# A chunked delta-rule recurrence inside a projection stage: the triangular inverse multiplied into its operand ahead of the chain, two matmul bursts a chunk in place of three

## The chip, the cores and the metric

The kernel runs on one core of a Trainium2 chip. The metric is the device time of one execution in microseconds; the number quoted is the median of three runs. TensorE (PE in the rows) does the matmuls, VectorE (DVE) and ScalarE (ACT) do elementwise work and empty PSUM, GpSimd (POOL) does small elementwise work, and SyncE (SP) issues the DMAs.

## The reference

One layer of a hybrid encoder on 528 prompt tokens (16 of them learned meta tokens) and 8 x 16 decode tokens, width 2048, all float32. What matters here is head group A, 16 heads of 64:

```python
h = rms_norm(x, norm_mix)
proj = h @ w_in                              # 2048 x 5408
...
def step(S, inp):                            # per head, S is 64 x 64
    r_t, w_t, k_t, v_t, a_t, b_t = inp
    sa = jnp.einsum('bhvk,bhk->bhv', S, a_t)
    S = S * w_t + sa * b_t + v_t * k_t       # outer products
    return S, jnp.einsum('bhvk,bhk->bhv', S, r_t)
...
x = x + concat(group_norm(y) * gate, conv_branch) @ w_out
x = x + (gelu(conv3(u)) * z) @ w_ffn_down    # [u, z] = rms_norm(x) @ w_ffn_up
```

## The kernel before

**Stages.** In order: load and normalise x; the input projection together with both head groups; the output projection; the feed-forward network (up, down), whose rows come from lines 1277 and 1361 (up) and 1581 and 370 (down); the final norm. The large matmuls split every float32 operand into a high and a low part and use three products (weight high x input high, weight high x input low, weight low x input high), all written by line 154 in the first two of these stages.

**The recurrence.** The 16 heads are worked on in 8 pairs; a pair's two heads sit on partitions 0 to 63 and 64 to 127, so that each small matmul is issued twice, once for each head (h = 0, 1). The tokens of a pair form 11 chunks of 64: chunks 0 and 1 are the decode tokens, chunks 2 to 10 the prompt. Within a chunk the recurrence is solved in closed form: with a unit triangular matrix and its inverse T (`tt`), computed ahead by `core_pre`, the state S of the chunk before gives

- z = (masked k a) v + a S, then u = T z (the correction that the chunk's tokens make to each other),
- y = r S + (masked k r) v + (masked b r) u, and the new S = decay (S + k v + b u).

`core(i)` is a generator that does this for pair i. Each of its steps issues a burst of 64x64 matmuls, then yields a number: how many large matmuls have to pass before its next step. Per chunk there are three bursts: one for z (ends with a copy of z by ScalarE into `zs`, line 871), one for u = T z (rows `g<-zs,tt`; copy into `us`, line 878), one for the new S and for y (copy into `S`, line 896). `prep(c0)` makes the masked products and the transposes for two chunks at a time in two PSUM banks; VectorE (lines 783, 784) and ScalarE (785, 786) copy them into the SBUF tile `slot`.

**What sets the order on TensorE.** From the second step of the stage on, TensorE's instructions stand as the program emits them. `tick()` is called after every large matmul; it advances the generators. The stream `st_b` holds the pairs' `core` generators, `st_p` the `core_pre` ones, `st_e` the group norms (`gn_gen`), others the elementwise chains. The other generators prefer to run where the chain has just issued a burst:

```python
while self.items and self.cnt <= 0 and (beside or self.poll or self.cnt <= -WAIT):
...
def tick():
    st_f.tick()
    beside = st_b.tick() or not st_b.items
    for st in streams:
        st.tick(beside)
```

So `beside` is true in the tick in which the chain issued a burst, or where no chain is left; without it another generator's step waits up to `WAIT` large matmuls beyond its own number. The order of the other engines is set by a scheduler at build time, with a bonus (`HPC`) for the chain's copies.

**PSUM.** `mb()` hands out two banks in turn. `prep` takes both; so do each part of `core_pre`, the state update of the decode chunks, the transposes of `gn_gen` (rows `mb<-consts,yb`), and one bank is taken by the squares in `gn_gen` (line 949, ScalarE writes it, VectorE sums it in line 951). Whoever takes a bank waits until its last user's copies are done. The chain itself accumulates in the tile `g`, in banks of its own.

Of the kernel before, what the change touches and what calls it, by code (L numbers as in the profile page):

```python
# [46 lines left out]
WAIT = 6  # L47
# [15 lines left out]
def hymba_stream_kernel(  # L63
# [305 lines left out]
    def mmx(o_, l_, r_, st_, sp_):  # L369
        nc.tensor.matmul(o_, l_, r_, start=st_, stop=sp_, skip_group_check=True)  # L370
# [376 lines left out]
    def core(i):  # L747
# [6 lines left out]
        RB, KA, RK, BT, VT, KT_ = range(6)  # L754

        def prep(c0):

            nch = min(2, NCH - c0)
            pss = [mb(), mb()]
            for z in range(nch):  # L760
                c = c0 + z
                o = 192 * z
                for h in range(2):
                    x, I = hs[h], ident[hs[h], hs[h]]
                    mmx(pss[h][ot[h], o:o + 128], ar[x, c, 3, :], ar[x, c, 0:2, :], z == 0, True)
                for h in range(2):
                    x, I = hs[h], ident[hs[h], hs[h]]
                    mmx(pss[h][x, o:o + 64], ar[x, c, 2, :], ar[x, c, 1, :], z == 0, True)
                for h in range(2):
                    x, I = hs[h], ident[hs[h], hs[h]]  # L770
                    mmx(pss[h][x, o + 64:o + 128], ar[x, c, 2, :], I, False, True)
                for h in range(2):
                    x, I = hs[h], ident[hs[h], hs[h]]
                    mmx(pss[h][ot[h], o + 128:o + 192], ar[x, c, 3, :], I, False, True)
                for h in range(2):
                    x, I = hs[h], ident[hs[h], hs[h]]
                    mmx(pss[h][x, o + 128:o + 192], vv[x, c * 64:c * 64 + 64], I, False, True)
            sl = rw.tile([P, 2, 6, 64], F32, tag="slot", name="slot", bufs=2)
            kind = int(c0 < 2)
            for h in range(2):  # L780
                pv = pss[h][:, 0:192 * nch].rearrange("p (z w t) -> p z w t", w=3, t=64)
                x, y = hs[h], ot[h]
                TT(sl[x, :nch, RB], pv[x, :, 0], mk[x, kind, 1].unsqueeze(1).to_broadcast([64, nch, 64]), ALU.mult)
                TT(sl[x, :nch, KA:KA + 2], pv[y, :, 0:2], mk[y, kind].unsqueeze(1).to_broadcast([64, nch, 2, 64]), ALU.mult)
                act(sl[x, :nch, BT:BT + 2], pv[x, :, 1:3], AF.Copy)
                act(sl[x, :nch, KT_], pv[y, :, 2], AF.Copy)
            slots[c0] = sl
            if c0 == NCH - 1:
                state["jit"] = i


        am = once("am", [P, 2, 576], 0.0)
        for c in range(2):
            for z in range(2):
                nc.gpsimd.tensor_copy(am[:, c, 256 * z:256 * z + 320].rearrange("p (q w) -> p q w", w=80)[:, :, 0:16],
                                      ar[:, c, z, :].rearrange("p (q j) -> p q j", j=16))
# [11 lines left out]
        for c in range(2):  # L808
            for h in range(2):
                mmx(g[hs[h], h, 64 * c:64 * c + 64], sl[hs[h], c, KA], sl[hs[h], c, VT], c == 0, False)  # L810
            for q in range(4):
                for h in range(2):
                    mmx(g[hs[h], h, 64 * c:64 * c + 64], am[hs[h], c, 64 * q:64 * q + 64], s0[hs[h], 4 * c + q, :], False, q == 3)
                for h in range(2):
                    mmx(g[ot[h], h, 64 * c:64 * c + 64], am[hs[h], c, 256 + 64 * q:320 + 64 * q], s0[hs[h], 4 * c + q, :], c == 0 and q == 0, False)
# [13 lines left out]
        for h in range(2):  # L829
            with ALL(offset=HPC):  # L830
                uv = g[hs[h], h, 128:256].rearrange("p (c v) -> p c v", c=2)
                act(us[hs[h]], uv, AF.Copy)
            for c in range(2):
                with ALL(offset=HPC):
                    TT(um[hs[h], c], uv[:, c].unsqueeze(1).to_broadcast([64, 4, 64]),
                       qm[hs[h]].unsqueeze(2).to_broadcast([64, 4, 64]), ALU.mult)
        yield Y_SU
# [17 lines left out]
        for c in range(2, NCH):  # L855
# [13 lines left out]
            for h in range(2):  # L869
# [3 lines left out]
            for h in range(2):  # L873
                mmx(g[hs[h], h, 64:128], tt[hs[h], c, :], zs[hs[h]], True, True)
# [4 lines left out]
            if z == 0 and c + 2 < NCH:  # L879
                prep(c + 2)  # L880
            yield Y_CU
# [11 lines left out]
            S2 = rw.tile([P, 64], F32, tag="S", name="S", bufs=3)  # L893
# [790 lines left out]
```

## Time and profile before

| | |
|---|---|
| median of three runs | 3164.76 us (3161.8 to 3167.85) |
| profiled execution: its own time | 3158.8 us |
| profiled execution: span from first to last instruction | 3157.0 us |
| TensorE busy | 3004.3 us, 95% |
| VectorE, ScalarE, GpSimd busy | 2304.7 (73%), 1484.1 (47%), 422.9 (13%) us |
| mean granted TensorE clock | 0.979 of 2.4 GHz |

The projection stages end at about 1344 us; the chains of the 8 pairs lie between about 293 and 1316 us. From 1344 us on the feed-forward network runs, which the change does not touch. Matmuls are pipelined, so a matmul's own duration in a row is longer than its distance to the next start; for large matmuls in a row the distance between two starts is the time that each one costs.

### The profile page before, as it was taken

The numbers are of one execution on the slowest core, as the hardware profiler recorded it, in microseconds if no ns is written. First come the engines' busy times: TensorE is split into PE (matmuls) and PEld (weight loads), VectorE is DVE, ScalarE is ACT, GpSimd is POOL, SyncE is SP. The second block draws the span as 40 slices with busy tenths as digits, with TensorE's granted clock in tenths as the row PEclk, the third lists the DMA queues.
The fourth block names the chain that finished last, engine by engine and source line by source line (L and its number), as shares of the span: only waits on it lengthen the run. The fifth ranks groups of instructions, "written<-read, shape, count | busy, mean of one in ns | idle before, by whom it ended". The sixth has DMA issues, their size and how long they took to land.

```text
span 3157.0 us, 63878 instructions
## 1 busy us (share of the span) xinstructions
PE 3004.3 (95%) x24566; PEld 2832.7 (90%) x24566; DVE 2304.7 (73%) x4341; ACT 1484.1 (47%) x3226; POOL 422.9 (13%) x848
## 2 busy tenths in 40 slices
PE   8998998999889999999999999999999999999998
PEld 6887887788768788899999999999999999999997
DVE  5778577766755443388888888888888888888877
ACT  6653544435455544464444444444444444444445
POOL 2124224043240321000000000000000000000001
PEclk9999999999879999999999999999999999999999
DMA  4652333143545433363333333333333375334325
GB/s 136 195 160 68 84 90 87 50 110 77 139 112 169 126 103 109 92 185 100 97 103 96 97 97 99 97 94 97 95 100 102 104 232 159 119 112 145 114 90 158
DMA packets 537644, 362.96 MB, mean 115 GB/s; under 512 B 80392, under 2 KB 506540, under 8 KB 536666
## 3 DMA queue, kind: packets, MB, share of 16 engines
q1 hardware_dynamic: 536682, 358.29, 39.0%
q8 instruction: 193, 3.16, 0.4%
q14 instruction: 113, 0.93, 0.1%
q0 software_dynamic: 656, 0.58, 0.1%
HBM read 294.71 MB, written 65.03 MB: 114 GB/s over the span
## 4 chain that ended last, share of the span: by engine, by line
PE 60%; DMA 5%; DVE 4%; POOL 3%; issue 2%; ACT 2%; SPq 1%; DVEq 0%; ACTq 0%; POOLq 0%
PE p_t L1361 20%; PE p_b L1361 15%; PE mm L154 13%; PE wb L370 9%; POOL tp L694 1%; POOL ttmp L692 1%; DMA ra<-in_w_ffn_down_dram 1%; PE mb L370 1%; PE g L370 1%; DMA wst<-in_w_ffn_down_dram 1%; DVE lo L1582 1%; DMA ct<-c_d 1%; DVE wlo L131 1%; PE pss L370 0%; DMA lp<-ld 0%
## 5 line engine op out<-in xcount | busy, mean ns | idle before, releaser
L1277 ACT ACTIVATE hi<-a 128x512 fp32r<-128x512 f32 x528 | 324.0, 630 | 448.7 <-PE p_b L1361 199.0
L154 PE MATMUL mm<-xh,whi 128*128 128x384 f32 (+2 forms) x1344 | 441.3, 328 | 10.4 <-ACT whi L129 8.6
L154 PE MATMUL mm<-xh,wlo 128*128 128x384 f32 (+2 forms) x1344 | 442.6, 330 | 7.1 <-DVE wlo L131 6.8
L1361 PE MATMUL p_t<-ht,hi 128*128 128x322 f32 x1408 | 441.1, 315 | 0.6 <-ACT hi L1277 0.6
L154 PE MATMUL mm<-xl,whi 128*128 128x384 f32 (+2 forms) x1344 | 440.4, 328 | 0.0
L1361 PE MATMUL p_t<-lt,hi 128*128 128x322 f32 x1408 | 436.5, 311 | 0.0
L1278 DVE TENSOR_TENSOR lo<-a,hi 128x512 fp32r<-128x512 f32 x528 | 352.0, 687 | 109.0 <-ACT hi L1277 79.5
L1361 PE MATMUL p_t<-ht,lo 128*128 128x322 f32 x1408 | 423.1, 312 | 0.0
L131 DVE TENSOR_TENSOR wlo<-wst,whi 128x512 fp32r<-128x512 f32 (+2 forms) x332 | 219.7, 662 | 208.3 <-ACT whi L129 186.2
L129 ACT ACTIVATE whi<-wst 128x512 fp32r<-128x512 f32 (+2 forms) x332 | 198.7, 600 | 255.1 <-PE mm L154 173.3
L154 PEld LDWEIGHTS mm<-xh,wlo 128*128 128x128 f32 (+1 forms) x1344 | 259.5, 193 | 21.3 <-DVE wlo L131 12.0
L154 PEld LDWEIGHTS mm<-xh,whi 128*128 128x128 f32 (+1 forms) x1344 | 259.3, 193 | 20.7 <-ACT whi L129 9.4
L1361 PEld LDWEIGHTS p_t<-ht,hi 128*128 128x128 f32 x1408 | 266.6, 189 | 3.2 <-ACT hi L1277 0.9
L154 PEld LDWEIGHTS mm<-xl,whi 128*128 128x128 f32 (+1 forms) x1344 | 260.3, 194 | 8.4 <-issue 1.8
L1361 PEld LDWEIGHTS p_t<-lt,hi 128*128 128x128 f32 x1408 | 266.7, 189 | 0.0
L1361 PEld LDWEIGHTS p_t<-ht,lo 128*128 128x128 f32 x1408 | 263.4, 190 | 0.4 <-DVE lo L1278 0.3
L1361 PE MATMUL p_b<-hb,lo 128*128 128x322 f32 x704 | 223.5, 317 | 0.0
L1361 PE MATMUL p_b<-lb,hi 128*128 128x322 f32 x704 | 219.6, 312 | 0.0
L1361 PE MATMUL p_b<-hb,hi 128*128 128x322 f32 x704 | 218.6, 311 | 0.0
L154 PE MATMUL mm<-g,whi 128*128 128x320 f32 (+2 forms) x960 | 210.3, 313 | 4.9 <-DVE fy L1495 2.4
L370 PE MATMUL wb<-t,hi 128*128 128x320 f32 x928 | 205.7, 310 | 0.0
L1581 ACT ACTIVATE hi<-ra 128x512 fp32r<-128x512 f32 x174 | 110.0, 632 | 195.4 <-PE wb L370 166.7
(515 smaller groups left out, 7164.3 us busy)
## 6 DMA issues: line engine op xcount, KB each, us to landing
a<-in_w_ffn_up_dram SPq DMA_DIRECT2D x352, 256.0 KB
wst<-in_w_in_dram SPq DMA_DIRECT2D x168, 256.0 KB
ra<-in_w_ffn_down_dram SPq DMA_DIRECT2D x58, 512.0 KB
gr<-g_d SPq DMA_DIRECT2D x84, 320.0 KB
wst<-in_w_ffn_down_dram SPq DMA_DIRECT2D x68, 256.0 KB
g_d<-uu SPq DMA_DIRECT2D x44, 320.0 KB
wst<-in_w_out_dram SPq DMA_DIRECT2D x48, 256.0 KB
ld<-lo_d SPq DMA_DIRECT2D x40, 192.0 KB
```

The source lines that it names most:

```text
L129: act(hi[:, :nk, :nc_], st[:, :nk, :nc_], AF.Copy)
L131: TT(lo[:, :nk, :nc_], st[:, :nk, :nc_], hi[:, :nk, :nc_].bitcast(F32), ALU.subtract)
L154: nc.tensor.matmul(o, w_, x_[kk][:, s0:s1], start=(kk == 0 and w_ is h and x_ is ah), stop=(kk == nk - 1 and w_ is l))
L370: nc.tensor.matmul(o_, l_, r_, start=st_, stop=sp_, skip_group_check=True)
L692: nc.gpsimd.tensor_tensor(tv, lp[:, s:s + 1, s + 1:32].to_broadcast([108, J, L]), tp[:, :J, s:s + 1].to_broadcast([108, J, L]), ALU.mult)
L694: nc.gpsimd.tensor_tensor(tp[:, :J, s + 1:32], tp[:, :J, s + 1:32], tv, ALU.add)
L1277: act(hi[:], v_, AF.Copy)
L1278: TT(lo[:], v_, hi[:].bitcast(F32), ALU.subtract)
L1361: nc.tensor.matmul(pr[op], w_[:, c], x_[z], start=(h == 0 and c == 0 and n == 0), stop=(h == 1 and c == 3 and n == 2))
L1581: act(hi[:], src, AF.Copy)
L1582: TT(lo[:], src, hi[:].bitcast(F32), ALU.subtract)
```

## The change

The inverse T is multiplied into a ahead of the chain: a new step `prep2` takes the slot that `prep` filled one chunk earlier, and computes, for two chunks at a time, zv = (masked k a) v and aT = a transposed times T, which two further copies by ScalarE put back into the slot (over KA and into the new field AT). The chain's first burst then gives u directly, u = T zv + aT S, and the burst for z, its copy `zs` and its `yield` are gone. `prep` gets one more transpose per chunk and head (that of a). On even chunks the first burst is followed by `prep` for the chunks two further on, on odd chunks by `prep2` for the next two. `WAIT` goes from 6 to 10. The tile `S` has 2 buffers in place of 3, the slot has 7 fields in place of 6, and the mask tile `am` is laid out flat.

```diff
-WAIT = 6
+WAIT = 10
...
-        RB, KA, RK, BT, VT, KT_ = range(6)
+        RB, KA, RK, BT, VT, AT, KT_ = range(7)
...
+                for d, w, l, r_ in ((1, p, 3, slice(0, 2)), (0, o, 2, 1), (0, o + 64, 2, None), (1, p + 128, 3, None),
+                                    (0, o + 128, -1, None), (0, o + 192, 0, None)):
+                    for h in range(2):
+                        x = hs[h]
+                        if l == 0 and c0 == 0:
+                            continue
...
+            kind, nt = int(c0 < 2), 3 if c0 else 2
...
+                act(sl[x, :nch, BT:BT + nt], px[:, :, 1:1 + nt], AF.Copy)
+                act(sl[x, :nch, KT_], py[:, :, 2], AF.Copy)
...
+        def prep2(c0):
+
+            nch, sl = min(2, NCH - c0), slots[c0]
+            pss = [mb(), mb()]
+            for z in range(nch):
+                for h in range(2):
+                    x = hs[h]
+                    mmx(pss[h][x, 128 * z:128 * z + 64], sl[x, z, KA], sl[x, z, VT], z == 0, True)
+                for h in range(2):
+                    x = hs[h]
+                    mmx(pss[h][x, 128 * z + 64:128 * z + 128], sl[x, z, AT], tt[x, c0 + z, :], False, True)
+            for h in range(2):
+                x = hs[h]
+                pv = pss[h][x, 0:128 * nch].rearrange("p (z w t) -> p z w t", w=2, t=64)
+                act(sl[x, :nch, KA], pv[:, :, 0], AF.Copy)
+                act(sl[x, :nch, AT], pv[:, :, 1], AF.Copy)
...
+        prep2(2)
         yield Y_SU
...
             for h in range(2):
-                mmx(g[hs[h], h, 0:64], sl[hs[h], z, KA], sl[hs[h], z, VT], True, S is None)
+                mmx(g[hs[h], h, 64:128], tt[hs[h], c, :], sl[hs[h], z, KA], True, S is None)
             if S is not None:
                 for h in range(2):
-                    mmx(g[hs[h], h, 0:64], ar[hs[h], c, 0, :], S[hs[h]], False, True)
+                    mmx(g[hs[h], h, 64:128], sl[hs[h], z, AT], S[hs[h]], False, True)
...
-            zs = rw.tile([P, 64], F32, tag="zs", name="zs", bufs=1)
-            for h in range(2):
-                with ALL(offset=HPC):
-                    act(zs[hs[h]], g[hs[h], h, 0:64], AF.Copy)
-            yield Y_C
-            for h in range(2):
-                mmx(g[hs[h], h, 64:128], tt[hs[h], c, :], zs[hs[h]], True, True)
...
-            if z == 0 and c + 2 < NCH:
-                prep(c + 2)
-            yield Y_CU
+            if c + 2 - z < NCH:
+                (prep2 if z else prep)(c + 2 - z)
+            yield Y_C
```

On TensorE, in the program's order before, one chunk of a late pair reads as follows between large matmuls (line 154): the burst for z, seven large matmuls, then the burst `g<-zs,tt` alone (`arbk` holds a and r, `tt` is T; one row of this order is two instructions in the trace).

```order
5748 L370 MATMUL g<-slot 64x64 x2
5749 L370 MATMUL g<-S,arbk_1950 64x64 x4
5750 L154 MATMUL mm<-c2l,whi 128x322
5751 L154 MATMUL mm<-c2h,wlo 128x322
5752 L154 MATMUL mm<-c3h,whi 128x322
5753 L154 MATMUL mm<-c3l,whi 128x322
5754 L154 MATMUL mm<-c3h,wlo 128x322
5755 L154 MATMUL mm<-c0h,whi 128x320
5756 L154 MATMUL mm<-c0l,whi 128x320
5757 L370 MATMUL g<-zs,tt_2585 64x64 x2
5758 L154 MATMUL mm<-c0h,wlo 128x320
```

In the program's order of the changed kernel an odd chunk of the same pair has this burst on TensorE (`mb<-slot` and `mb<-tt,slot` are `prep2`, `mb<-consts,yb` are the transposes of the group norm).

```order
6033 L154 MATMUL mm<-c0l,whi 128x320
6034 L370 MATMUL g<-slot,tt_2623 64x64 x2
6035 L370 MATMUL g<-S,slot 64x64 x2
6036 L370 MATMUL g<-S,arbk_1950 64x64 x2
6037 L370 MATMUL mb<-slot 64x64 x2
6038 L370 MATMUL mb<-tt_2623,slot 64x64 x2
6039 L370 MATMUL mb<-slot 64x64 x2
6040 L370 MATMUL mb<-tt_2623,slot 64x64 x2
6041 L370 MATMUL mb<-consts,yb_14229 64x64 x12
6042 L154 MATMUL mm<-c0h,wlo 128x320
```

The row `g<-zs,tt` with its own place between large matmuls is gone, and the group norm's transposes, which also use the two `mb` banks, now stand directly behind `prep2`.

ScalarE's order around the same place in the changed kernel, from the even chunk's `prep` on (lines 781 and 782 are the copies of `prep`, 801 and 802 those of `prep2`, 956 the squares of the group norm, 903 the copy of S, 885 that of u, 970 the group norm's output).

```order
1222 L781 ACTIVATE slot<-mb 64x2x192
1223 L782 ACTIVATE slot<-mb 64x2x64
1224 L781 ACTIVATE slot<-mb 64x2x192
1225 L782 ACTIVATE slot<-mb 64x2x64
1226 L956 ACTIVATE mb<-yb_14229 128x384
1227 L903 ACTIVATE S<-g,pc 64x64 x2
1228 L959 ACTIVATE gs<-gs,eps 128x6
1229 L885 ACTIVATE us<-g 64x64 x2
1230 L801 ACTIVATE slot<-mb 64x2x64
1231 L802 ACTIVATE slot<-mb 64x2x64
1232 L801 ACTIVATE slot<-mb 64x2x64
1233 L802 ACTIVATE slot<-mb 64x2x64
```

Here the squares (line 956) stand ahead of the copy of S, and the four copies of `prep2` behind the copy of u. Before, at this place of the pair, a copy `zs` stood between the squares and the group norm's square root, and the copy of S before the squares.

## Rows read from the trace of the kernel before

**Rows 1.** The page: TensorE's busy share in 40 equal slices of 79 us, in tenths, and the granted clock in tenths.

```profile
PE   8998998999889999999999999999999999999998
PEclk9999999999879999999999999999999999999999
```

**Rows 2.** Busy time by stretch: the stage with the chains, then the feed-forward network's up part. Columns: stretch, its length, then busy us (instructions) of PE, PEld, DVE, ACT, POOL, the granted clock, DMA share, GB/s.

```profile
237.00:1344.00 1107.00, 1006.86 (x11304) 884.95 (x11302) 656.20 (x1363) 519.11 (x1362) 287.52 (x614) 0.95 0.37 101
1344.00:2538.00 1194.00, 1188.89 (x7979) 1174.97 (x7978) 993.88 (x1736) 542.13 (x961) 63.02 (x96) 1.00 0.35 104
```

**Rows 3.** Who waited for whom, TensorE, 237 to 1344 us. Columns: total us, times, longest.

```profile
PE mb L370 <- ACT slot L786: 15.4, 18, 4.4
PE g L370 <- ACT S L896: 13.8, 10, 8.4
...
PE mm L154 <- DVE wlo L131: 8.4, 16, 1.0
PE mb L370 <- DVE gs L951: 7.2, 2, 3.8
PE mb L370 <- DVE slot L784: 6.5, 7, 1.6
PE g L370 <- ACT zs L871: 4.7, 5, 3.6
```

**Rows 4.** TensorE in order of time, two bursts of a late pair among large matmuls: start us, duration us, instruction, count.

```profile
1292.94 0.31 PE L154 MATMUL mm<-y1h,whi 128*128 128x322 f32 x1
1293.09 0.31 PE L154 MATMUL mm<-y1l,whi 128*128 128x322 f32 x1
1293.33 0.33 PE L370 MATMUL g<-zs,tt 64*64 64x64 f32 x4
1293.59 0.41 PE L154 MATMUL mm<-y1h,wlo 128*128 128x322 f32 x1
1293.84 0.31 PE L154 MATMUL mm<-y2h,whi 128*128 128x322 f32 x1
...
1294.59 0.31 PE L154 MATMUL mm<-y3h,wlo 128*128 128x322 f32 x1
1294.82 0.36 PE L370 MATMUL g<-slot 64*64 64x64 f32 x8
1294.99 0.22 PE L370 MATMUL g<-S,consts 64*64 64x64 f32 x2
1295.01 0.26 PE L370 MATMUL g<-us,slot 64*64 64x64 f32 x2
1295.05 0.23 PE L370 MATMUL g<-S,consts 64*64 64x64 f32 x2
1295.10 0.28 PE L370 MATMUL g<-us,slot 64*64 64x64 f32 x6
1295.32 0.41 PE L154 MATMUL mm<-y0h,whi 128*128 128x320 f32 x1
1295.57 0.31 PE L154 MATMUL mm<-y0l,whi 128*128 128x320 f32 x1
```

**Rows 5.** The instructions that use the tile `zs`: count, duration ns min/median/max, first and last start. (352 of them, because the decode chunks of every pair, which keep their own z step, use the name too: 176 rows of the program's order at two instructions each, 32 of them of the decode chunks.)

```profile
L370 PE MATMUL g<-zs,tt x352: 218/218/366, 303.9 to 1311.9; 64*64 64x64 f32 x176
```

**Rows 6.** ScalarE's groups, 200 to 1360 us: count, then busy us and mean ns of one, then idle before.

```profile
L785 ACT ACTIVATE slot<-mb 64x256 f32<-64x256 f32 (+1 forms) x96 | 34.5, 360 | 47.0 <-DVE slot L784 39.2 <-PE mm L154 2.8 <-PE g L370 2.0
L871 ACT ACTIVATE zs<-g 64x64 f32<-64x64 f32 x144 | 31.2, 217 | 48.0 <-PE g L370 46.4
L786 ACT ACTIVATE slot<-mb 64x128 f32<-64x128 f32 (+1 forms) x96 | 25.3, 263 | 1.2
L949 ACT ACTIVATE mb<-yb 128x384 f32<-128x384 f32 (+1 forms) x16 | 7.3, 459 | 5.3 <-DVE yb L946 5.3
```

**Rows 7.** TensorE in order of time at three places where `core_pre` takes the two `mb` banks directly behind a `prep`: the last matmuls of the first `prep`, then for each place the first matmul behind it. In brackets: idle us before, and who ended it.

```profile
363.39 0.28 PE L370 MATMUL mb<-consts,vv 64*64 64x64 f32 x4
365.53 0.32 PE L370 MATMUL mb<-arbk 64*64 64x64 f32 x2 [1.85 <-ACT slot L786]
...
1029.24 0.47 PE L370 MATMUL mb<-arbk 64*64 64x64 f32 x2 [2.55 <-ACT slot L786]
...
1152.29 0.32 PE L370 MATMUL mb<-arbk 64*64 64x64 f32 x2 [1.63 <-DVE slot L784]
```

**Rows 8.** TensorE in order of time at other waits for the `mb` banks: the second `prep` of a pair, 8 large matmuls behind its first (two rows); a `prep` behind the squares of the group norm (two places); the group norm's transposes, 14 large matmuls behind a `prep`.

```profile
574.95 0.43 PE L370 MATMUL mb<-arbk 64*64 64x128 f32 x2 [1.01 <-DVE slot L784]
575.71 0.32 PE L370 MATMUL mb<-arbk 64*64 64x128 f32 x3 [0.34 <-ACT slot L786]
...
492.25 0.45 PE L370 MATMUL mb<-arbk 64*64 64x128 f32 x3 [3.35 <-DVE gs L951]
...
917.31 0.47 PE L370 MATMUL mb<-arbk 64*64 64x128 f32 x3 [3.82 <-DVE gs L951]
...
927.92 0.47 PE L370 MATMUL mb<-consts,yb 64*64 64x64 f32 x2 [4.37 <-ACT slot L786]
```

**Rows 9.** In order of time from one `prep` to the next chunk's first burst: the last matmuls of the `prep`, ScalarE's copy of S, and the burst that waited for it.

```profile
596.11 0.28 PE L370 MATMUL mb<-consts,vv 64*64 64x64 f32 x4
...
599.67 0.63 ACT L896 ACTIVATE S<-g,pc 64x64 f32<-64x64 f32 x2
...
600.36 0.27 PE L370 MATMUL g<-slot 64*64 64x64 f32 x2 [0.58 <-ACT S L896]
```

More of the change, by code (lines that the diff above doesn't have):

```diff
@@ L761, in prep @@
                 c = c0 + z
-                o = 192 * z
-                for h in range(2):
-                    x, I = hs[h], ident[hs[h], hs[h]]
-                    mmx(pss[h][ot[h], o:o + 128], ar[x, c, 3, :], ar[x, c, 0:2, :], z == 0, True)
-                for h in range(2):
[L767 to L779, printed above, removed]
+                o, p = 256 * z, 192 * z
@@ new lines, in prep @@
+                for d, w, l, r_ in ((1, p, 3, slice(0, 2)), (0, o, 2, 1), (0, o + 64, 2, None), (1, p + 128, 3, None),
[4 more added lines that the diff above has]
+                            continue
+                        lhs = vv[x, c * 64:c * 64 + 64] if l < 0 else ar[x, c, l, :]
+                        rhs = ident[x, x] if r_ is None else ar[x, c, r_, :]
+                        n = 128 if isinstance(r_, slice) else 64
+                        mmx(pss[h][ot[h] if d else x, w:w + n], lhs, rhs, z == 0 and w == 0, True)
@@ L780, in prep @@
+            sl = rw.tile([P, 2, 7, 64], F32, tag="slot", name="slot", bufs=2)
+            kind, nt = int(c0 < 2), 3 if c0 else 2
             for h in range(2):
-                pv = pss[h][:, 0:192 * nch].rearrange("p (z w t) -> p z w t", w=3, t=64)
                 x, y = hs[h], ot[h]
-                TT(sl[x, :nch, RB], pv[x, :, 0], mk[x, kind, 1].unsqueeze(1).to_broadcast([64, nch, 64]), ALU.mult)
-                TT(sl[x, :nch, KA:KA + 2], pv[y, :, 0:2], mk[y, kind].unsqueeze(1).to_broadcast([64, nch, 2, 64]), ALU.mult)
@@ L785, in prep @@
-                act(sl[x, :nch, BT:BT + 2], pv[x, :, 1:3], AF.Copy)
-                act(sl[x, :nch, KT_], pv[y, :, 2], AF.Copy)
+                px = pss[h][x, 0:256 * nch].rearrange("p (z w t) -> p z w t", w=4, t=64)
+                py = pss[h][y, 0:192 * nch].rearrange("p (z w t) -> p z w t", w=3, t=64)
+                TT(sl[x, :nch, KA:KA + 2], py[:, :, 0:2], mk[y, kind].unsqueeze(1).to_broadcast([64, nch, 2, 64]), ALU.mult)
+                TT(sl[x, :nch, RB], px[:, :, 0], mk[x, kind, 1].unsqueeze(1).to_broadcast([64, nch, 64]), ALU.mult)
@@ L789, in prep @@
                 state["jit"] = i
-        am = once("am", [P, 2, 576], 0.0)
+        def prep2(c0):
[13 more added lines that the diff above has]
+                act(sl[x, :nch, AT], pv[:, :, 1], AF.Copy)
+        am = once("am", [P, 1088], 0.0)
         for c in range(2):
             for z in range(2):
-                nc.gpsimd.tensor_copy(am[:, c, 256 * z:256 * z + 320].rearrange("p (q w) -> p q w", w=80)[:, :, 0:16],
+                nc.gpsimd.tensor_copy(am[:, 512 * c + 256 * z:512 * c + 256 * z + 320].rearrange("p (q w) -> p q w", w=80)[:, :, 0:16],
                                       ar[:, c, z, :].rearrange("p (q j) -> p q j", j=16))
@@ L812, in core @@
                 for h in range(2):
-                    mmx(g[hs[h], h, 64 * c:64 * c + 64], am[hs[h], c, 64 * q:64 * q + 64], s0[hs[h], 4 * c + q, :], False, q == 3)
+                    mmx(g[hs[h], h, 64 * c:64 * c + 64], am[hs[h], 512 * c + 64 * q:512 * c + 64 * q + 64], s0[hs[h], 4 * c + q, :], False, q == 3)
                 for h in range(2):
-                    mmx(g[ot[h], h, 64 * c:64 * c + 64], am[hs[h], c, 256 + 64 * q:320 + 64 * q], s0[hs[h], 4 * c + q, :], c == 0 and q == 0, False)
+                    mmx(g[ot[h], h, 64 * c:64 * c + 64], am[hs[h], 512 * c + 256 + 64 * q:512 * c + 320 + 64 * q], s0[hs[h], 4 * c + q, :], c == 0 and q == 0, False)
         zs = rw.tile([P, 2, 64], F32, tag="zs", name="zs8", bufs=1)
@@ L861, in core @@
             for h in range(2):
-                mmx(g[hs[h], h, 0:64], sl[hs[h], z, KA], sl[hs[h], z, VT], True, S is None)
+                mmx(g[hs[h], h, 64:128], tt[hs[h], c, :], sl[hs[h], z, KA], True, S is None)
             if S is not None:
                 for h in range(2):
-                    mmx(g[hs[h], h, 0:64], ar[hs[h], c, 0, :], S[hs[h]], False, True)
+                    mmx(g[hs[h], h, 64:128], sl[hs[h], z, AT], S[hs[h]], False, True)
                 for h in range(2):
                     mmx(g[ot[h], h, yc], ar[hs[h], c, 1, :], S[hs[h]], True, False)
-            zs = rw.tile([P, 64], F32, tag="zs", name="zs", bufs=1)
-            for h in range(2):
-                with ALL(offset=HPC):
-                    act(zs[hs[h]], g[hs[h], h, 0:64], AF.Copy)
-            yield Y_C
-            for h in range(2):
-                mmx(g[hs[h], h, 64:128], tt[hs[h], c, :], zs[hs[h]], True, True)
             us = rw.tile([P, 64], F32, tag="us", name="us", bufs=1)
@@ L892, in core @@
                 mmx(g[ot[h], h, yc], sl[hs[h], z, RB], us[hs[h]], False, True)
-            S2 = rw.tile([P, 64], F32, tag="S", name="S", bufs=3)
+            S2 = rw.tile([P, 64], F32, tag="S", name="S", bufs=2)
             for h in range(2):
```

## The prediction, on record before the run

> **What bounds the kernel now.** I read the page's slices first. TensorE is busy for 90% or more in nearly every slice from about 1400 us on; the holes lie before that, and there alone does its clock fall [rows 1]. By stretch: in 237 to 1344 us, where the eight chains run, TensorE is busy for 1006.9 of 1107 us at a mean clock of 0.95 of 2.4 GHz; in the up part it is busy for 1188.9 of 1194 us [rows 2]. VectorE (656 us) and ScalarE (519 us) are at 59% and 47% of the chain stretch. So the stage goes at TensorE's speed: its large matmuls, the small bursts between them, and 100 us in which it stands still. The table of waits says what for: nearly all for the chain's tiles and the `mb` banks, only 8.4 us for the low half of a weight [rows 3]. The chain itself is hidden: between two bursts TensorE does large matmuls, and counted in the program's order there are 5568 of them before the feed-forward network, with and without the change; the last pair's chain ends some 150 of them before the end in both. A shorter chain therefore ends nothing earlier. What counts is what a burst costs TensorE, and where it waits.
>
> **What a burst costs.** Large matmuls of this shape start 0.15 us apart (1292.94, 1293.09). Around the burst `g<-zs,tt` of 4 instructions, 0.75 us pass from 1293.09 to 1293.84; less two large matmuls that is 0.45 us. Around the chain's last burst of 20 instructions, 1294.59 to 1295.57 less 0.30 gives 0.68 us [rows 4]. Sixteen more instructions cost 0.23 us, so 0.0144 us each, and a burst costs 0.45 - 4 x 0.0144 = 0.39 us merely for being there.
>
> **The sum, part by part.**
>
> *Bursts that go.* The 72 prompt chunks (8 pairs of 9) lose one each: 288 of the 352 instructions in [rows 5]. The wider `WAIT` merges two more: in the program's order, runs of small matmuls between large ones go from 439 to 365. 74 x 0.39 = -28.9 us.
>
> *Instructions that come.* Per chunk, the burst `g<-zs,tt` takes 4 with it, `prep2` brings 8 for zv and aT, of which the 4 for zv only replace those of the old z burst, whose place T zv takes, and `prep` brings 4 for the transpose: net 8 per chunk, 576 in all (288 more rows in the program's order). 576 x 0.0144 = +8.3 us. A rule of the Trainium skill speaks against that price: TensorEngine Tiling (Array Packing), Instruction Overhead, gives each matmul about 60 cycles however few columns it has, 25 ns at 2.4 GHz. By it this term would be an estimated 14.4 us; the row shows less, and I keep the row.
>
> *ScalarE.* 144 copies `zs` go (31.2 us); 160 copies of 64x128 or less come, at most 160 x 0.263 = 42.1 us, and the wider copies of `prep` add 0.10 us each (0.36 against 0.26 for 128 columns more), some 8 us [rows 6]. Plus 19 us on 519 of 1107: hidden by ScalarE's own idle time, and at worst the 19 us, were it full.
>
> *Waits that go.* For `zs` 4.7 us. For the squares' bank 7.2 us: the two places are a `prep` 10 large matmuls behind the squares [rows 8]; now the next taker, `prep2`, comes 18 behind. For the slot's copies 21.9 us are on record (15.4 and 6.5) [rows 3]. Of these, the second `prep` of each pair behind the first stays, 8 x (1.01 + 0.34) = 10.8, and so do the three places where `core_pre` follows a `prep`, 6.0 [rows 7, 8]; the other 5.1, mostly the 4.37 us of the group norm's transposes, goes, because those now stand elsewhere. Together -17.0 us. At least nothing goes, if other takers wait in their place.
>
> *Waits that come.* With two takers per two chunks where there was one, and `WAIT` holding the others back until the chain has just issued, takers of the two banks stand directly behind each other: counted in the program's order, the group norm's transposes behind `prep2` in seven pairs, `core_pre` behind `prep2` twice, one more `core_pre` behind a `prep`, one group norm behind `core_pre`. Each must wait until four copies are done. From above, the same place behind a `prep` costs 1.63 to 2.55 us [rows 7], but there VectorE's masking comes first; from below, one pair of ScalarE copies, 0.5 us [rows 6]. `prep2` needs no VectorE but ScalarE has the two copies of u ahead (0.44) and then four of 0.26: 1.5 us. I take 1.6 for the nine and 2.0 for the two: +18.4 us (5.5 to 28). In each pair the squares now stand ahead of the copy of S on ScalarE, 0.46 us [rows 6] that the chain's next burst waits for: 8 x 0.46 = +3.7 (from 0, where something else was waited for anyway). `prep2(2)` stands between the decode chunks' u and the state update: its four copies are about as long as the large matmuls there, so 0.3 us a pair, +2.4 (0 to 8).
>
> Sum: -28.9 + 8.3 - 17.0 + 18.4 + 3.7 + 2.4 = -13.1 us. The profiled execution took 3158.8 us, so 3145.7; the median of the runs stands 6.0 above it, which gives 3152 us for a median.
>
> Its ends: with the waits that come at their least and all those named going, -28.9 + 8.3 - 17.0 + 5.5 = -32 us; with none of the old waits going and the new at their most, -28.9 + 8.3 + 28 + 3.7 + 8 = +19 us.
>
> **The rivals.** What a measurement of this kernel can tell from no change is about 0.2%, 6.3 us.
>
> *It is handed back, no change.* Either the new bank waits cost 2.5 us each (+9), or TensorE, faster by 20 us, runs into VectorE, which splits the weights and runs the convolution taps: for that speak the slices in which it is busiest, against it that only 8.4 us of 1107 were spent waiting for a low half [rows 3]. With half of the burst saving lost, -13 + 10 = -3: about 3162 us.
>
> *Slower: `prep2` finds the slot not filled.* Before, a slot was read two chunks after its `prep`; now `prep2` reads it one chunk after, 18 large matmuls. In [rows 9] `prep` ends at 596.4, the next chunk's first burst starts at 600.36 after waiting 0.58 for S, which ScalarE copied right behind the slot's copies. Without that wait it would have started at 599.78, and the slot was ready at 599.67: a margin of 0.1 us where VectorE was in the middle of its taps. There are 40 `prep2`. The case decides from an average of 13/40 = 0.33 us each upwards; at 0.8 us it is +32 - 13 = +19: 3184 us. Against it: the wait for S ends at the same moment, so the first part of such a wait is already paid; and in the later pairs there are no taps. The Trainium skill has the same warning in TensorEngine Tiling (Array Packing), PSUM Bottleneck: tiling quickens TensorE but not the emptying of PSUM, which may become the bottleneck; whether it does here, the trace of before cannot show.
>
> *More than forecast.* After each wait of 3 to 4 us the clock falls to its lower level of 1.2 GHz, which the page shows as the 7 and 8 in the clock's row [rows 1]. Four such waits are among those that go (the three long ones of [rows 8], and the 3.6 us for `zs` in [rows 3]), the new ones are shorter. If the clock stays up, 12 to 20 us more: 3136 us.
>
> **How the numbers follow.** The forecast with its own range of 3141 to 3162 has 0.52; handed back 0.22; slower 0.13; more 0.13. The range from 3132 to 3169 leaves out the far half of slower, the far end of more and some of the tails of the others, about 2 in 10. Faster by over 0.2% is below 3158.4: most of the first case and all of the last, 0.64; within, 0.23; slower, 0.13.
>
> **What would show it.** In the changed profile: no `zs` in the prompt chunks; two bursts a chunk; TensorE busy about 20 us less in the chain stretch; waits of the group norm's transposes for a copy of `prep2`, seven times 1.3 to 2 us; none for the squares' sum. The prediction is wrong if `prep2` itself, or the chain's first burst behind it, waits for `slot` by more than 10 us in all, if large matmuls wait for weights more than before, or if long waits, and with them the lower clock, appear at new places.

## The result, and the profile after

The changed kernel takes 3192.83 us (3187.37 to 3196.57) against 3163.28 us (3158.53 to 3167.85) for the kernel before on the same chip: a ratio of 1.0095, 95% interval 1.0082 to 1.0107, so 30 us slower. The forecast was 3152 us, in a range of 3132 to 3169.

The page of the changed kernel: TensorE's total, its busy share in 40 slices of 80 us, the granted clock. They answer to [rows 1].

```profile
PE 2995.3 (94%) x25142; PEld 2849.9 (89%) x25142; DVE 2305.0 (72%) x4341; ACT 1492.8 (47%) x3241; POOL 402.1 (13%) x848
...
PE   8998898898788899999999999999999999999998
...
PEclk9999998999898999999999999999999999999999
```

TensorE is busy for 9 us less (2995.3 against 3004.3 us) in a span that is 28.6 us longer, and its clock now falls below 9 tenths in three slices in place of two. By stretch, the answers to [rows 2]:

```profile
237.00:1372.00 1135.00, 993.79 (x11818) 895.67 (x11817) 652.10 (x1353) 524.13 (x1371) 268.27 (x615) 0.94 0.36 98
1372.00:2566.00 1194.00, 1188.58 (x7980) 1175.01 (x7979) 992.38 (x1732) 542.42 (x960) 63.10 (x94) 1.00 0.35 104
```

The up part is as it was. The stage with the chains ends 28 us later although TensorE is busy 13 us less in it: it stands still for 141 us in place of 100. For whom it waits there, the answer to [rows 3]:

```profile
PE g L370 <- ACT S L903: 21.4, 14, 6.7
PE mm L154 <- DVE wlo L131: 14.8, 10, 8.8
PE mb L370 <- ACT slot L782: 13.7, 17, 2.7
PE g L370 <- ACT us L885: 11.9, 4, 6.9
PE mb L370 <- DVE um L848: 11.7, 5, 7.2
PE mb L370 <- DVE yb L961: 10.2, 4, 5.2
PE mb L370 <- DVE slot L780: 9.4, 5, 3.3
PE g L370 <- ACT zs L832: 9.3, 4, 3.9
PE ma L1025 <- POOL cn L1021: 8.0, 2, 4.2
...
PE mb L370 <- ACT slot L802: 4.6, 5, 1.5
```

And three rows of the kernel before that [rows 3] does not show:

```profile
PE mb L370 <- DVE yb L954: 3.8, 1, 3.8
PE g L370 <- ACT us L878: 2.0, 2, 1.1
PE ma L1018 <- POOL cn L1014: 0.5, 2, 0.3
```

The wait for `zs` in the prompt chunks is gone (what stays, L832, is the decode chunks', 4.6 us before). The waits that the forecast priced highest, those behind `prep2`'s copies, are the last row: 4.6 us. What grew are mostly few and long waits: for S (13.8 before), for `us` (2.0), for a low half of a weight (8.4 before, none longer than 1.0; now one of 8.8), for the group norm's `yb` (3.8), for the convolution's `cn` (0.5).

For all kernels below, the profiled execution is split at the last matmul of the output projection. In the kernel before that matmul ends at 1405.2 us; the 1344 us given ahead of the prediction as the end of the projections lie 61 us too early. Behind it every kernel takes 1745 to 1753 us. The time up to it is divided into TensorE's idle time (the stretch less its busy time), its busy time counted at full clock ("work"), and what the lower clock adds to that.

| us | ends at | idle | work | lower clock |
|---|---|---|---|---|
| before | 1405.2 | 123.6 | 1232.8 | 48.8 |
| changed | 1437.0 | 161.4 | 1222.7 | 52.8 |
| difference | +31.8 | +37.8 | -10.1 | +4.0 |

So there are two questions: why the work fell by 10 us and not by the 20.6 of the sum (-28.9 + 8.3), and where 38 us of idle time come from in place of the sum's 7.5 (-17.0 + 18.4 + 3.7 + 2.4).

### The profile page after: what moved, and what is told of

It reads as the page before. It is cut to its first block, busy times and chain, and to the rows that moved or that the text cites. A ratio compares the mean times of both kernels' runs of the same rounds, so it can differ in the third digit from the quotient of the medians.

```text
span 3185.6 us, 65033 instructions
## 1 busy us (share of the span) xinstructions
PE 2995.3 (94%) x25142; PEld 2849.9 (89%) x25142; DVE 2305.0 (72%) x4341; ACT 1492.8 (47%) x3241; POOL 402.1 (13%) x848
## 4 chain that ended last, share of the span: by engine, by line
PE 52%; DMA 3%; DVE 2%; ACT 1%; issue 1%; SPq 0%; DVEq 0%; ACTq 0%
PE p_t L1368 20%; PE p_b L1368 15%; PE mm L154 8%; PE wb L370 8%; DMA ra<-in_w_ffn_down_dram 2%; DVE lo L1589 1%; DMA wst<-in_w_ffn_down_dram 1%; PE pss L370 0%; DMA gr<-g_d 0%; DVE s L1579 0%; PE g L370 0%; PE mb L370 0%; DVE acc L1567 0%; DVE wlo L131 0%; DMA a<-in_w_ffn_up_dram 0%
```

## The experiments

Every kernel was timed beside the kernel before on the same chip; over the chips used, the median of the kernel before ranged from 3155 to 3163 us. Gains and losses below are therefore differences of the ratios, at 3160 us. The last three columns come from one profiled execution each, which lay up to 10 us above or below the median of its kernel, so a few us of idle time say nothing. The table has all kernels; "td" means that POOL issues the store and the reload of the inverse, "act" or "actfirst" that `prep`'s copies stand ahead of its maskings.

| run | median us | ratio to before (95%) | idle | work | lower clock |
|---|---|---|---|---|---|
| after_wait6 | 3203.9 | 1.0146 (1.0130 to 1.0162) | 165.8 | 1228.1 | 63.4 |
| before_wait10 | 3165.0 | 1.0024 (1.0014 to 1.0034) | 139.0 | 1229.6 | 38.9 |
| before_shift1 | 3164.2 | 1.0016 (1.0006 to 1.0027) | 133.6 | 1231.9 | 50.2 |
| before_shift2 | 3162.1 | 1.0010 (1.0001 to 1.0019) | 133.5 | 1232.8 | 40.6 |
| after_shift1 | 3198.3 | 1.0126 (1.0112 to 1.0139) | 169.4 | 1226.8 | 53.1 |
| after_shift2 | 3192.8 | 1.0111 (1.0095 to 1.0127) | 165.6 | 1222.1 | 62.7 |
| after_td_pool | 3159.8 | 1.0003 (0.9993 to 1.0013) | 135.3 | 1220.5 | 49.6 |
| before_td_pool | 3137.7 | 0.9937 (0.9925 to 0.9949) | 112.7 | 1231.6 | 38.6 |
| after_td_cs18 | 3157.0 | 1.0002 (0.9994 to 1.0011) | 131.8 | 1223.8 | 53.4 |
| after_td_off | 3155.0 | 0.9992 (0.9984 to 1.0001) | 140.3 | 1213.3 | 57.0 |
| after_td_nop2 | 3135.2 | 0.9932 (0.9919 to 0.9945) | 139.6 | 1200.4 | 49.1 |
| after_td_wait6 | 3182.0 | 1.0074 (1.0062 to 1.0086) | 147.8 | 1226.5 | 55.6 |
| after_td_actfirst | 3147.6 | 0.9975 (0.9966 to 0.9984) | 131.2 | 1221.5 | 46.8 |
| before_td_actfirst | 3117.1 | 0.9883 (0.9866 to 0.9900) | 101.4 | 1229.6 | 42.8 |
| after_td_prio | 3171.1 | 1.0047 (1.0031 to 1.0063) | 145.9 | 1217.6 | 65.3 |
| before_td_act_w10 | 3154.9 | 0.9987 (0.9975 to 0.9999) | 129.6 | 1226.4 | 43.4 |
| after_td_act_late | 3119.8 | 0.9876 (0.9855 to 0.9897) | 115.6 | 1222.0 | 35.0 |
| after_late | 3166.7 | 1.0023 (1.0011 to 1.0035) | 140.4 | 1224.8 | 49.6 |

### Is it the wider wait?

```
-WAIT = 10        (after_wait6)          -WAIT = 6         (before_wait10)
+WAIT = 6                                +WAIT = 10
```

> The changed kernel with WAIT back at 6; the two bursts a chunk and the new prep2 stay. Theory W (the other generators' steps, held back up to ten ticks and then issued in one heap behind a burst, queue up on ScalarE and VectorE ahead of the chain's next copy): the 30 us that the change cost go, 3160 to 3168 us, and the waits for S, us and um together fall from 45 us to below 30. Theory P (the pace: a chunk in 18 ticks instead of 25, with one copy round less, leaves the in-order engines too little time): 3185 to 3197 us, no change. Theory D (reloads from DRAM come late because the queue of SP stands at the store of the inverse): a shift of either sign by some 10 us, since the order on SP moves a little, and a wait of 7 to 9 us at a reload of a spilled tile stays.

> The kernel before with WAIT = 10 alone, three bursts a chunk. Theory W: it becomes slower, by 15 to 30 us (3178 to 3193). Theory P: 3160 to 3166, as before. Theory D: within 10 us of before.

It was the first suspect, and the times speak against it: with `WAIT` back at 6 the changed kernel is 16 us slower still, and in the kernel before `WAIT = 10` costs 8 us. The wider `WAIT` lowers the work by 5 us in the changed kernel and by 3 in the kernel before, as bursts merge.

### Is it an accident of the order?

```
before_shift1: Y_CU 7 -> 6, Y_CS 11 -> 12        after_shift1: Y_C 7 -> 8, Y_CS 11 -> 10
before_shift2: Y_JT 8 -> 10                      after_shift2: Y_JT 8 -> 10
```

> The kernel before with the chain's last burst of a chunk one large matmul earlier (Y_CU 6, Y_CS 12; a chunk still takes 25 ticks): no instruction, burst or copy comes or goes. Theory T (the long waits are collisions of work on in-order engines, which the pauses of the kernel before happen to miss and any other order meets): slower by 6 to 25 us, 3164 to 3183, with TensorE idle for 110 to 130 us in the stretch from 237 us where it was 104. Theory M (the added idle time is caused by an edit of the change): within 5 us of before.

> The kernel before with each chain begun later by four large matmuls (Y_JT 10 in place of 8, used twice); nothing comes or goes. Theory T: slower by 6 to 25 us. Theory M: within 5 us of before.

> The changed kernel with the second burst of a chunk one large matmul later (Y_C 8, Y_CS 10; a chunk still takes 18 ticks). Theory T: it may go either way by 5 to 25 us from 3193, and as the changed kernel has had no choice of its pauses, rather down. Theory M: within 5 us of 3193.

> The changed kernel with each chain begun later by four large matmuls (Y_JT 10). Theory T: either way by 5 to 25 us from 3193. Theory M: within 5 us of 3193.

The times move by 3 to 5 us in the kernel before and by 5 to 10 in the changed one (idle time by 4 to 10 in either), and the gap between the two stays, at 32 and 35 us. So none of these four shifts makes the loss, but a shift alone can move idle time by a quarter of the 38 us.

### The queue of SP

Two of the longest waits of the changed kernel begin outside the chain. `tp` is the inverse while POOL computes it, `td` its copy in DRAM, `tt` the inverse as the chain reads it, and `sp_d` a DRAM buffer into which tiles `w` are spilled. In order of time: SP's queue with the last step of the inverse on POOL, then what ScalarE did.

```profile
961.50 0.42 SPq L548 DMA_DIRECT2D ld<-lo_d  x1
...
968.36 0.23 POOL L694 TENSOR_TENSOR tp<-tp,ttmp 108x16 f32<-108x16 f32 x1
...
968.62 1.80 SPq L696 DMA_DIRECT2D td<-tp  x2
...
973.00 1.86 SPq L698 DMA_DIRECT2D tt<-td  x4
...
975.41 0.93 SPq L566 DMA_DIRECT2D w<-sp_d  x2
...
978.02 0.88 ACT L636 ACTIVATE vv<-w 128x384 f32<-128x384 f32 x2 [9.45 <-DMA w<-sp_d]
978.91 0.45 ACT L885 ACTIVATE us<-g 64x64 f32<-64x64 f32 x2
```

SP stands still for 6.7 us, because the next in its queue is the store of the inverse, which POOL has not finished. Behind it stands the reload of a spilled v. ScalarE, in order too, waits 9.45 us for that reload, and behind `vv` stands the chain's `us`: TensorE waits 6.9 us for it. At 847.7 us it is VectorE that waits for another late reload:

```profile
847.69 0.56 DVE L587 TENSOR_TENSOR arbk<-w,ld 128x384 f32<-128x384 f32 x1 [10.89 <-DMA w<-sp_d]
```

SP had stood still for 18.2 us at the store of another inverse, until 822.78 us, and came to this reload, behind all that had piled up, at 845.39 us. TensorE waits 8.8 us for the `wlo` behind it. Together these are 15.7 us that the kernel before does not have.

```
-                nc.sync.dma_start(td[:]...            (both stores of the inverse)
+                nc.gpsimd.dma_start(td[:]...
-                nc.sync.dma_start(tt[32 * q:...       (its four reloads)
+                nc.gpsimd.dma_start(tt[32 * q:...
```

> The changed kernel with the two stores of the inverse (td<-tp) and its four reloads (tt<-td) issued by POOL, which computes the inverse, in place of SP: SP's queue no longer stands still for 98 us in all at the store. Theory D: the late reloads of spilled tiles (VectorE idle 10.9 us before an arbk product, ScalarE idle 9.5 us before vv) go, and with them 15 to 25 us: 3168 to 3178 us. Theories W and P: less than 8 us, 3185 to 3197.

> The same two lines moved to POOL in the kernel before, where SP stands at that store for 86 us in all but no reload of a spilled tile is waited for by more than 5.3 us. Theory D: a gain of 0 to 10 us, less than in the changed kernel. Theories W and P: the same shift in both kernels, within 6 us.

29 us go in the changed kernel and 20 us in the kernel before, in both more than expected. In the changed one idle time falls by 26 us, and the longest waits for `us` and `wlo` fall to 3.3 and 1.7 us, so the theory holds for the two waits. What both kernels gain comes at least in part from another effect of the same queue, which was not foreseen: the loads of the weights stand in it too. ScalarE's wait for them, in the kernel before and in the changed one:

```profile
ACT whi L129 <- DMA wst<-in_w_in_dram: 38.0, 8, 10.3
```

```profile
ACT whi L129 <- DMA wst<-in_w_in_dram: 43.6, 9, 11.3
```

With the store on POOL this wait is gone in both, and TensorE's wait for the high halves behind it falls from 8.6 and 7.9 us to 0 and 1.5. The repair takes 9 us off the gap; 21 us stay.

### What prep2 costs

```
after_td_off:   aT written to pss[h][ot[h], 64*z:...] (the other half of the partitions) in place of pss[h][x, ...]
after_td_nop2:  prep2 returns at once, so that neither of its products is formed
after_td_cs18:  Y_CS 11 -> 18
after_td_wait6: WAIT 10 -> 6
```

> As after_td_pool, but prep2 writes aT into the other half of the partitions, so that its instructions alternate between four 64x64 parts of the array in place of two; nothing else differs. In the trace of the changed kernel prep2 adds 16 instructions and 0.465 us to a burst, 29 ns each, where the instructions of the chain's 20-instruction burst cost 14.4. If the price hangs on how many parts alternate: 40 bursts times 16 times 0.0146 = 9 us less, about 3150 us, and such a burst shrinks from 1.04 to 0.81 us. If prep2's instructions cost 29 ns wherever they are put: 3157 to 3163 us.

> As after_td_pool with prep2 left out altogether (no matmuls, no copies, no banks; the chain reads the masked products as they stand, so z and aT are not multiplied by the inverse). Its own matmuls are worth 40 x 0.465 = 18.6 us. Theory Q (its copies and banks make others wait): another 12 to 25 us go, 3116 to 3129 us. Theory P: only the matmuls, 3138 to 3146 us.

> The changed kernel with the inverse's store and reload on POOL (3159.8 us), and with Y_CS raised from 11 to 18, so that a chunk again takes 25 ticks, as before the change. The kernel before with the same store on POOL took 3137.7 us; 25.6 of these 22 us lie in TensorE standing still between 237 us and the end of the projections out. Theory P (the shorter chunk leaves the copies too little time): the waits for S, slot and us fall by 12 us or more in all, 3140 to 3150 us. Theory Q (prep2 as such: its four copies on ScalarE, its two banks, its matmuls): no gain, 3157 to 3165 us.

> As after_td_pool with WAIT = 6. In the changed kernel as it stands WAIT = 6 cost 11 us more. If that is the bursts that the wider wait merges (a tick and its fixed price each) the same shows here: 3167 to 3174 us. If it was the order on SP that moved with it, which this kernel is less open to: 3155 to 3165 us.

A burst with `prep2` in the changed kernel, and below it the same burst in after_td_off, TensorE in order of time:

```profile
625.39 0.29 PE L154 MATMUL mm<-xh,wlo 128*128 128x272 f32 x1
625.61 0.27 PE L370 MATMUL g<-slot,tt 64*64 64x64 f32 x2
...
625.77 0.28 PE L370 MATMUL g<-S,slot 64*64 64x64 f32 x4
625.89 0.28 PE L370 MATMUL mb<-slot 64*64 64x64 f32 x4
...
626.24 0.28 PE L370 MATMUL mb<-tt,slot 64*64 64x64 f32 x4
626.45 0.39 PE L154 MATMUL mm<-xh,whi 128*128 128x272 f32 x1
```

```profile
619.51 0.29 PE L154 MATMUL mm<-xh,wlo 128*128 128x272 f32 x1
619.72 0.28 PE L370 MATMUL g<-slot,tt 64*64 64x64 f32 x2
...
620.18 0.23 PE L370 MATMUL mb<-slot 64*64 64x64 f32 x2
620.33 0.39 PE L154 MATMUL mm<-xh,whi 128*128 128x272 f32 x1
```

From the start of the last large matmul to that of the next are 1.06 us in the one (625.39 to 626.45) and 0.82 in the other (619.51 to 620.33): four instructions of `prep2` take 0.116 us, 29 ns each, when they alternate between two 64x64 parts of the array, and 14.4 ns, the price in [rows 4], when they use four. The work falls by 7.2 us (expected 9); the time falls by 3.5 us, with intervals that overlap. Without `prep2` the work falls by 20.1 us and the time by 22, but idle time is no shorter (139.6 against 135.3), and TensorE still waits 22.1 us for S: `prep2`'s banks and copies make nobody wait longer in sum.

A chunk of 25 ticks in place of 18 leaves the time as it is, and a chain that is 63 large matmuls longer in each pair ends nothing later, as the forecast had said. But the waits behind that total change. First after_td_pool, then after_td_cs18:

```profile
PE g L370 <- ACT S L903: 20.8, 15, 6.0
PE ma L1025 <- POOL cn L1021: 7.0, 2, 4.2
```

```profile
PE ma L1025 <- POOL cn L1021: 20.7, 3, 14.5
PE g L370 <- ACT S L903: 2.3, 2, 2.0
```

With the old pace the wait for S all but goes, so the shorter chunk does carry it; what was gained is lost at other places, most of it in one wait of 14.5 us for `cn`. That wait is no matter of the pace: the same transpose of the convolution, near 400 us, waits 14.2 to 16.7 us in four of the kernels here (before_wait10, after_shift2, after_td_cs18, before_td_act_w10), 3.8 us in the changed kernel and at most 0.3 in the kernel before. Totals of kernels that met it and kernels that missed it cannot be compared to better than that. `WAIT = 6` costs 22 us here, as little explained as the 16 above.

### ScalarE behind the maskings

The changed kernel in order of time, from one chunk's last burst to the next chunk's first:

```profile
489.38 0.28 PE L370 MATMUL g<-us,slot 64*64 64x64 f32 x6
...
490.38 0.75 DVE L1041 SCALAR_TENSOR_TENSOR acc<-cbt,parD,acc 128x514 f32<-128x514 f32 x1
...
492.40 0.43 DVE L779 TENSOR_TENSOR slot<-mb,mk 64x256 f32<-64x256 f32 x1
492.84 0.28 DVE L780 TENSOR_TENSOR slot<-mb,mk 64x128 f32<-64x128 f32 x1
493.21 0.48 ACT L781 ACTIVATE slot<-mb 64x384 f32<-64x384 f32 x1 [5.47 <-DVE slot L780]
...
494.01 0.63 ACT L903 ACTIVATE S<-g,pc 64x64 f32<-64x64 f32 x2
...
494.69 0.37 PE L370 MATMUL g<-slot,tt 64*64 64x64 f32 x2 [3.16 <-ACT S L903]
```

The burst that gives S is through at 489.7, but ScalarE copies S at 494.01: it stands at `prep`'s copy, which is issued ahead of that of S and waits for VectorE's masking of the same slot, and the masking stands behind taps of the convolution (`acc`). ScalarE's own waits in 237 to 1380 us:

```profile
ACT slot L781 <- DVE slot L780: 58.0, 27, 8.4
```

Before it was 39.2 us [rows 6]. Three ways to take this away: the copies ahead of the maskings, both at the chain's priority, and the calls moved behind the copy of S.

```
actfirst:  act(sl[.., BT:BT + nt], ..); act(sl[.., KT_], ..)   now ahead of   TT(sl[.., KA:KA + 2], ..); TT(sl[.., RB], ..)
prio:      the four of them under  with ALL(offset=HPC):
late:      -            if c + 2 - z < NCH:                     (behind the copy of us, first burst)
           -                (prep2 if z else prep)(c + 2 - z)
                        yield Y_C
                        ...
                        S = S2
           +            if c + 2 - z < NCH:                     (behind the copy of S, second burst)
           +                (prep2 if z else prep)(c + 2 - z)
```

> As after_td_pool (3159.8 us), with prep's two ScalarE copies issued ahead of VectorE's two maskings of the same bank instead of behind them. In the changed kernel's trace ScalarE stands still for 58.0 us (27 times, longest 8.4) at a copy into slot until a masking on VectorE has ended, which itself stands behind the convolution's taps; in the kernel before 39.2 us (27 times, longest 2.9). Theory S (the added waits are ScalarE blocked there, with the copies us and S and the weights' high halves behind it): this wait goes and TensorE's idle time in the stretch falls by 10 to 20 us, 3140 to 3150 us. Theory V (VectorE's backlog of taps is itself what is waited for, and the masking then comes no earlier): 3155 to 3163 us.

> The same swap in before_td_pool (3137.7 us), where the longest such wait of ScalarE was 2.9 us. Theory S: a gain of 3 to 8 us at most, less than in the changed kernel. Theory V: within 4 us.

> As after_td_pool, with prep's maskings and copies raised to the priority of the chain's copies, so that they stand ahead of taps and weight halves in VectorE's and ScalarE's queues. Theories S and V both: the maskings no longer wait behind taps, and the waits for slot, S and us fall by 12 to 25 us, 3135 to 3148 us. If neither (the taps and weights that now stand behind are late in their turn): 3155 to 3165 us.

> after_td_actfirst (3147.6 us) with prep and prep2 called in the second burst of a chunk, behind the copy of S, in place of the first, behind the copy of us; matmuls and copies are the same, prep2 still comes 18 ticks behind prep. If the rest of the loss is that their copies stand between the chain's two copies: the waits for S (10.9 us) and us (5.2) go and the kernel takes 3130 to 3140 us. If the place makes no difference, because the copies wait for VectorE's taps wherever they stand: 3143 to 3152 us.

> The changed kernel as it stands (3193 us), inverse on SP and maskings ahead of the copies as before, with the calls of prep and prep2 alone moved from a chunk's first burst to its second. In the kernel with the two repairs this gained 28 us. If the place is what the change itself lost by: 3160 to 3172 us, about as long as before the change. If the place counts only once the repairs are made, and SP and the maskings dominate before: 3178 to 3193 us.

Copies first gain 9 us in the changed kernel, and 17 in the kernel before, where 3 to 8 were expected: ScalarE was blocked there as well, so this is a cost of both kernels and not what sets them apart. With both repairs in both, the gap is 30 us again (3147.6 against 3117.1 us). What differs is what the copies first leave. TensorE's wait for S, in before_td_actfirst and then in after_td_actfirst:

```profile
PE g L370 <- ACT S L896: 0.3, 1, 0.3
```

```profile
PE g L370 <- ACT S L903: 10.9, 6, 6.6
```

The priority costs 14 us, and the wait for S stays (24.9 us); why was not looked into further. The later place gains 31 us in the repaired kernel, where 8 to 18 were expected, and 23 us in the changed kernel as it stands: 3166.7 us, 0.2% above the kernel before. In the repaired kernel some 16 of the 27 us up to the last matmul of the output projection are idle time and 12 the lower clock. TensorE's longest waits in after_late, and then the page's clock row of after_td_act_late:

```profile
PE mb L370 <- ACT slot L782: 16.6, 22, 3.5
PE mm L154 <- DVE wlo L131: 14.6, 14, 3.9
PE ma L1025 <- POOL cn L1021: 12.7, 2, 9.0
```

```profile
PEclk9999999999999999999999999999999999999999
```

The waits of the chain's bursts for S (21.4) and of the group norm for `yb` (10.2) are gone. In the repaired kernel no slice is left below 9.

```
-WAIT = 6          (before_td_act_w10, on before_td_actfirst)
+WAIT = 10
```

> before_td_actfirst (3117.1 us) with WAIT = 10 alone. Its counterpart with the whole change took 3147.6 us. In the plain kernels WAIT = 10 raised TensorE's idle time from 123.6 to 139.0 us, while two shifts that only move the chain by a tick or four raised it to 133.5. If WAIT carries the rest of the loss: 3127 to 3137 us. If it is a shift like the others: 3116 to 3126 us.

33 us slower, more than either case allowed. A large part is one wait, at the transpose named above:

```profile
394.06 2.52 POOL L698 DMA_DIRECT2D tt<-td  x4 [3.14 <-DMA td<-tp]
...
397.04 0.30 POOL L1014 COPY cn<-cbt 128x128 f32<-128x128 f32 x1
...
397.39 0.48 PE L1018 MATMUL ma<-consts,cn 128*128 128x128 f32 x1 [16.68 <-POOL tp L687]
```

TensorE stands 16.68 us at a transpose of the convolution whose operand POOL copies only after the inverse and, here, after the stores and reloads that the repair put on POOL. That is over half of the 28 us of idle time that came. In before_wait10, where POOL issues neither, the same transpose waits 14.5 us and the kernel loses 8 us. So this run doesn't show that `WAIT` carries the loss in the kernels as they were; nor does it rule out a part of it, since at `WAIT = 10` in both the repaired kernels lie within 4 us of each other (3154.9 and 3147.6 us).

## Why the prediction was wrong, step by step

**What bounds the kernel** was right: TensorE's work and its holes in the stage with the chains. The chain's length counts for nothing in the total (after_td_cs18), but its pace counts in what it waits for: 20.8 us for S at 18 ticks a chunk, 2.3 at 25.

**Bursts that go, -28.9:** right in kind. The work fell.

**Instructions that come, +8.3:** mis-sized. All were priced at the 14.4 ns of the 20-instruction burst, in which four parts of the array alternate. `prep2`'s alternate between two: 0.465 us for 16, and without `prep2` the work falls by 20.1 us. The rule that I set aside, about 60 cycles for each instruction (the Trainium skill, TensorEngine Tiling (Array Packing), Instruction Overhead), which is 25 ns at 2.4 GHz, was near for these, at 29 ns, and far off for the burst that I took the price from, at 14.4. The sum by rows would have been: `prep2` 32 x 0.465 + 8 x 0.23 (those of a single chunk) = 16.7, `prep`'s new transposes 0.23 for two chunks (a burst with `prep` takes 0.93 us more than one without, 0.70 before), 8.3 in all, less the 4 instructions of each old z burst, 4.1: +21 in place of +8.3. With it the two terms give -8; measured is -10.1. So this took half of the 20.6 us that the work was to fall by.

**ScalarE, hidden:** the step that failed. It was costed as busy time (19 us more, of an engine busy for 47%), and the rows that showed the danger were in hand: 39.2 us of ScalarE's idle time lay in front of `prep`'s copies [rows 6], S was already waited for 13.8 us [rows 3], and of [rows 9], which was read for the slot, the forecast itself says that ScalarE copied S right behind the slot's copies. That the engine is idle there doesn't mean that it is free: it is blocked at the head of its queue, and the copy of S stands behind. This wait of ScalarE's grew to 58.0 us, and the chain, with 7 large matmuls fewer in a chunk, comes sooner to the copies behind it. The sum has no term for this. The runs show its size only together with the rest: 23 us go in the changed kernel when the calls of `prep` and `prep2` stand behind the copy of S.

**Waits that go, -17.0:** `zs` went (4.7); the squares' wait fell from 7.2 to 1.0; the slot's did not (21.9 before, 13.7 + 9.4 now). So 11 of 17.

**Waits that come, +18.4 +3.7 +2.4:** the wrong place. Banks behind `prep2` cost 4.6 us, and the state update waits no longer for `um` than before (11.7 against 12.3). The squares' 3.7 us was the one item that named a wait for S: S costs 7.6 us more, though at the place shown above it is `prep`'s copy that stands ahead and not the squares. The rest is not in the sum at all: the two late reloads (15.7), `yb` (10.2 against 3.8), `cn` (8.0 against 0.5), the decode chunks' `zs` (9.3 against 4.6).

**The rivals:** the slower case, 3184 us, came near in its number by luck, for its mechanism didn't come: neither `prep2`'s matmuls nor a burst behind them waited for an unfilled slot (the rows of `mb` with `slot` are `prep`, `core_pre` and the group norm's transposes waiting for banks). The case of a clock that stays up didn't come either: the lower clock costs 4 us more than before. It took the shorter waits to leave the clock up, but in the kernel before the granted clock is at its lower level, 1.2 GHz, behind the waits of 2.55 and 1.63 us of [rows 7] too. Of the signs that I gave for a wrong prediction two came true, weights waited for longer (8.4 to 14.8 us) and long waits with a lower clock at new places.

**What stays open.** Three causes of idle time were each taken away, and each gained 9 to 31 us in the changed kernel. Two of them, SP's store and the maskings, cost the kernel before 20 and 17 us as well, and with both away the gap is what it was, so they don't account for the 30 us. The later place of `prep` and `prep2` brings the changed kernel back to 0.2% above the kernel before. The same move was not tried in the kernel before, where `prep` also stands ahead of the copy of S. The traces bound what it could give there once the two repairs are made: TensorE waits for S and `us` together for 2.4 us in before_td_actfirst and for 16.1 us in after_td_actfirst. So the place is the likeliest cause of most of the gap, but without that run it is not shown; in the kernel before as it stood, with 13.8 us of waits for S, the move may gain too. Of the other edits, S with 2 buffers in place of 3 was not tried alone; in either kernel ScalarE's copies of S wait for the matmuls of `g` alone, 36.8 us before and 31.7 after. Why `WAIT = 6` makes the two-burst chain slower and `WAIT = 10` the three-burst one was not settled.

**Faster than both** are before_td_actfirst (3117.1 us) and after_td_act_late (3119.8 us), each 1.2% below the kernel before and alike within their intervals. On these repairs the multiplied-in inverse, at 8 us less work, wins nothing measurable over the old chain.

## What to carry to other kernels

An engine's busy share says whether its work fits, not whether a copy comes in time: for every instruction that is added ahead of one on the critical path, look up what the added one waits for, since an in-order engine hands that wait on to all behind it. The same holds for a DMA queue: a store that waits for a long computation belongs in the queue of the engine that computes, unless others stand behind it there. Price small matmuls from a burst that uses the same parts of the array as the new ones.

## What the runs showed of the hardware

64x64 matmuls cost 14.4 ns each where four parts of the array alternate and 29 ns where two do (0.82 against 1.06 us for the same 28 instructions). TensorE's granted clock did not simply follow the sum of the holes: after_td_act_late, with 115.6 us of idle time, has no slice below 9 tenths, while before_td_actfirst, with 101.4 us, has two and the changed kernel, with 161.4 us, three.
